# Moving projection groups inside a hybrid decoder layer: between the quarters of the merge, in pairs around the chain's steps, and a new order of the tail

## The chip, the cores and the metric

The kernel runs on one core of a Trainium2 chip. The metric is the device time of one execution in microseconds (us), as the median of several runs. TensorE does the matmuls and is PE in the rows; its weight loads are PEld. VectorE is DVE, ScalarE is ACT, GpSimd is POOL, and SyncE (SP) issues the transfers. TensorE's clock has two levels, 2.4 GHz and 1.2 GHz, and the profile gives the granted share: 1.00 is the full clock, 0.50 the half clock.

## The reference

One decoder layer on x of 512 x 1024 in float32. One input projection feeds two groups of heads, whose outputs are gated, joined and projected back:

```python
h = rms_norm(x, g_pre[l])
proj = h @ w_in[l]                                   # 512 x 1024 times 1024 x 4224
y_r = rwkv7_time_mix(p_rwkv, ...)                    # 8 heads of 64: a recurrence over 512 steps
q, k, v = jnp.split(p_attn, 3, axis=-1)
y_a = moba_attention(q, k, v)                        # 8 heads of 64: causal softmax, ALiBi, blocks of 256
y = jnp.concatenate([y_r, y_a], axis=-1) * jax.nn.silu(gates)
o = y @ w_out[l]
x = x + rms_norm(o, g_post[l])
```

The recurrence of one RWKV head, with a 64 x 64 state S, is

```python
Sa = jnp.einsum('bhij,bhj->bhi', S, a_t)
S = S * w_t[:, :, None, :] + Sa[..., None] * b_t[:, :, None, :] + v_t[..., None] * k_t[:, :, None, :]
y = jnp.einsum('bhij,bhj->bhi', S, r_t)
```

At 512 positions and blocks of 256 the attention of a query sees every earlier block, so the kernel computes plain causal attention with ALiBi.

## The kernel before

**Products in three parts.** Every large product splits its operands in two rounded halves (`hi`, `lo`) and adds hi x hi, hi x lo and lo x hi. The input projection makes 128 output columns at a time for all 512 positions: over two halves of the 1024 rows, three products of four matmuls (128 x 128 weights, 512 columns). Such a set of four matmuls is called a **projection group**, P, here; in the rows it is `ps_p<-xhi_r,whi`, `ps_p<-xhi_r,wlo` or `ps_p<-xlo_r,whi`, 128x512 x4. Its weights arrive over SP's queue as `wraw`, ScalarE rounds them to `whi`, VectorE subtracts to `wlo`. `PLAN` lists the pieces in order: keys (k), receptances (r) and values (v) of the RWKV pairs, V of the attention, then queries (q), attention keys (c) and gates (G).

**The stages.** After the first projections comes the *preparation* (`rwkv_keys`, `rwkv_pairs`, `rwkv_values`; four pairs of heads each): `rwkv_keys` makes two rank products of 128x512 on `ps_c` (`ps_c<-qx,V_r`; called K), norms, four transposes and the tiles AR, BK, E; `rwkv_pairs` transposes BK into BT (four 128 x 128 transposes on `ps_r`, called TB) and multiplies BK with AR (eight matmuls on `ps_s`, called A), in two halves per pair. `rwkv_inverse` then inverts the 32 x 32 triangular blocks on VectorE, moves them through DRAM, and merges them into 64 x 64 blocks on TensorE: two quarters of 32 matmuls of 32x32 for the first product (`ps_c<-BK_f,Am_f`) and two for the second (`ps_c<-Am_f,BK_f`). This is the *merge*. `rwkv_chain` walks eight chunks of 64 positions in sequence. A step of it runs on TensorE: F, 16 matmuls `ps_s<-E,AR_f` and `ps_r<-E,AR_f` that need the state of the step before; a copy of their result on ScalarE and one on VectorE; u, 8 matmuls `ps_c<-UV_f,Am_f`; copies of u; X, 16 matmuls `ps_s`/`ps_r<-UV_f,Am_f` that prepare the next chunk; D, 8 matmuls `ps_c<-UV_f,BT_f`, which needs the copies of u and gives the next state; Y, 8 matmuls of the output. The trace records each of these small float32 matmuls (32x32, 64x64, 64x128) as two, so that F has x32 there and the first product of the merge x128. Then follow the norm (`rwkv_norm`), the attention of four pairs of heads (`attn_pair`: scores, the row maxima on VectorE at L707, exponentials on ScalarE at L736, products with the values), the gating (`gates`, `gated`) and the output projection. The output is made in nine pieces, each from two **half** outputs of 12 matmuls: `half(i, 0)` over the RWKV heads and `half(i, 1)` over the attention heads.

**What sets the order.** The order of TensorE's instructions is written by a small planner at build time. `stream(projections())` emits one projection group at a time; after each, `side` lets other generators (the flows) emit a step, at most three per group, and at most two once the chain has ended. A flow says with `yield ns, wait` how much TensorE time the planner books for what it has just emitted and how long after that it wants not to be called. If no projection may be emitted, `drain` lets the clock jump to the earliest flow and takes one step at a time. `PENDING` is how many pieces past `q1` may be emitted before the chain has ended. These times are the planner's only; they make no wait on the chip. The engines run their instructions in the order written, and wait only for data and for buffers: PSUM banks are rings by tag (`PS`: two "p", three "s", two "c", one "r").

**The end.** `out_weights` brings the output weights (two of 256 KB per call of `wout`); `early_out` gates the RWKV heads and emits `half(0, 0)` and `half(1, 0)` among the attention; after all flows have ended, `half(i, 0)` of pieces 2 to 4 follow, and then the loop over the pieces, which emits `half(i + 5, 0)` ahead of `half(i, 1)`, sums squares on ScalarE (L910) and multiplies by g_post on VectorE (L913).

Of the kernel before, what the change touches and what calls it, by code (L numbers as in the profile page):

```python
# [39 lines left out]
PLAN = "k1 r1 k2 r2 k3 r3 v1 v2 v3 V q0 c0 G4 G5 q1 c1 q2 c2 G6 q3 c3 G7 G0 G1 G2 G3"  # L40
PENDING, AHEAD = 8, 5
MM = 232.0
# [3 lines left out]
def hybrid_layer(ctx, tc, x, xt, params, ranks, w_in, w_v, w_out, g_post, out):  # L46
# [53 lines left out]
    clock, flows, ready = [0.0], [], {}  # L100
# [258 lines left out]
    def rwkv_keys(p, ps):  # L359
# [4 lines left out]
        nc.scalar.activation(sq, k, AF.Square, scale=col(KK + p))  # L364
        yield 0, 0 if p else 4000
        th = []
# [23 lines left out]
        nc.scalar.activation(en, L, AF.Exp, scale=-1.0)  # L390
        yield 4 * MM, 5500

# [30 lines left out]
    def rwkv_pairs(p, ps):  # L423
# [7 lines left out]
        nc.vector.tensor_mul(ar[:, :, 1, :], v3(r), E[:, :, 1:C + 1])  # L431
        yield 0, max(4000, since[p] + 13000 - clock[0])
        msk = flat(mask).unsqueeze(1).to_broadcast([128, 4, 128])
        for c0 in (0, 4):
            ps = mps("r")
            for c in range(4):
                tr(ps[:, 128 * c:128 * c + 128], flat(BK[:, c0 + c]))
            acp(bt[:, c0:c0 + 4, :], ps.rearrange("p (c n) -> p c n", c=4))
            yield 900, 0
            pe = [mps("s") for _ in range(2)]  # L440
            for c in range(4):
                for e in range(2):
                    h = slice(64 * e, 64 * e + 64)
                    mm(pe[e][:, 128 * c:128 * c + 128], flat(BK[h, c0 + c]), flat(ar[h, c0 + c]), start=True, stop=True)
            for e in range(2):
                nc.vector.tensor_mul(am[:, e, c0:c0 + 4].rearrange("p c a b -> p c (a b)"),
                                     pe[e].rearrange("p (c n) -> p c n", c=4), msk)
            if c0:
                for hf in range(2):
                    d = slice(32 * hf, 32 * hf + 32)  # L450
                    nc.sync.dma_start(bd[hf, p].rearrange("n s t -> s n t"),
                                      am[d, :, :, 0, d].rearrange("s e c t -> s (e c) t"))
                paired[p] = True
            yield 1800, 2200
# [27 lines left out]
    def rwkv_inverse():  # L482
# [31 lines left out]
        for g in range(2):  # L514
# [6 lines left out]
            for e in range(2):  # L521
                (acp, vcp)[e](xq[32:64, 2 * g:2 * g + 2, e], px[64 * e + 32:64 * e + 64])
            yield 1700, 0
        for g in range(2):
# [6 lines left out]
            for q in range(2):  # L531
                for e in range(2):
                    (acp, vcp)[e](Am[2 * g + q][0:32, e, :, 0, 32:64], px[64 * e:64 * e + 32, q])
            yield 1700, 0
        ready["inverse"] = True
# [6 lines left out]
    def rwkv_chain():  # L542
# [20 lines left out]
        for c in range(NCH):  # L563
# [7 lines left out]
            vcp(uv[lo, 1], ry[1][hi])  # L571
            yield 900 * (c > 0), 700
            u = mps()[:, 0:NP * HD].rearrange("p (q i) -> p q i", i=HD)
# [4 lines left out]
            if not last:  # L578
                rn = values_in(c + 1)
            yield 500 + 1000 * (not last), 100  # L580
            if not last:
# [226 lines left out]
    def out_weights():  # L808
        for k in range(8):
            while not attended(*(((0, 1),) * 4 + ((0, 1, 2),) * 2 + ((0, 1, 2, 3),) * 2)[k]):  # L810
                yield 0, 300
            wout(k)
            ready["wout"] = k
            yield 0, 1500

# [17 lines left out]
    def early_out():  # L833
# [5 lines left out]
        for p in range(NP):  # L839
            gated(p, bonus[p])  # L840
        yield 0, 8000
        for i in range(2):
# [53 lines left out]
    for b in range(NB):  # L896
# [3 lines left out]
        os = [at() for _ in range(2)]  # L900
        for j, i in enumerate(mine):
            if i + AHEAD < len(pieces):
                for n in half(i + AHEAD, 0):
                    pass
            for n in half(i, 1):
                pass
            cs = slice(*pieces[i][1])
# [74 lines left out]
```

## Time and profile before

| | |
|---|---|
| runs | 385.98, 386.14, 391.16 us; median 386.14 us |
| profiled execution | 386.54 us, of which the span of its instructions is 384.8 us |
| granted TensorE clock over the span | 0.964 |
| busy | PE 358.9 us (93%), DVE 243.7 (63%), ACT 189.3 (49%), POOL 32.8 (9%) |
| transfers | 31.93 MB, mean 83 GB/s |
| projection groups in the stream | 600 matmuls `ps_p`, 58.3 + 57.9 + 56.9 us busy |
| chain that ended last | PE 80%, ACT 7%, DVE 6%, issue 3% |

The busy times are sums over the whole span; the engine that waits changes from stage to stage, so that the stages have to be read one by one. Matmuls overlap in the records: of four matmuls of 128x512 the row shows about 1.08 us, and the next row starts 0.92 us after it.

### The profile page before, as it was taken

What the parts mean: (1) busy time and instruction counts of PE and PEld (TensorE: products, weight loads), DVE (VectorE), ACT (ScalarE), POOL (GpSimd) and SP (SyncE); (2) the same over time, 40 slices, a digit from 0 to 9 for tenths busy, and PEclk for the clock granted to TensorE, in tenths of its full rate; (3) what the DMA queues carried; (4) which work ended last, traced back from release to release, by engine and by line L of the source; (5) the groups of instructions that cost most, each with busy time, mean ns of one, the idle gap of its engine ahead of it and who ended that gap; (6) DMA issues with size and microseconds to landing.
All of it is one profiled execution on the core that took longest, in us unless ns stands there. A gap on an engine that the chain in (4) does not pass through costs nothing.

```text
span 384.8 us, 7040 instructions
## 1 busy us (share of the span) xinstructions
PE 358.9 (93%) x2765; PEld 287.1 (75%) x2765; DVE 243.7 (63%) x521; ACT 189.3 (49%) x351; POOL 32.8 (9%) x55
## 2 busy tenths in 40 slices
PE   7999798999999999989999998889999989799893
PEld 3688576888877888877777775668888867688783
DVE  5976579859985999723544456884657961520344
ACT  5948855666654344632332357756457263510322
POOL 6000130012000000300000006222200000000000
PEclk9999998999999999976999996999999999989997
DMA  6830121321243223832111100110124401220334
GB/s 196 326 112 26 55 56 44 72 103 47 71 115 81 99 62 106 205 98 56 55 43 46 56 29 31 55 55 29 55 81 138 139 0 36 96 89 2 106 111 137
DMA packets 28321, 31.93 MB, mean 83 GB/s; under 512 B 12608, under 2 KB 15424, under 8 KB 28288
## 3 DMA queue, kind: packets, MB, share of 16 engines
q1 hardware_dynamic: 28288, 31.49, 27.0%
q8 instruction: 21, 0.34, 0.4%
q14 instruction: 12, 0.10, 0.1%
HBM read 28.07 MB, written 3.41 MB: 82 GB/s over the span
## 4 chain that ended last, share of the span: by engine, by line
PE 80%; ACT 7%; DVE 6%; issue 3%; DMA 1%; SPq 1%; POOL 1%; DVEq 0%; ACTq 0%
PE ps_p L92 38%; PE ps_s L92 23%; PE ps_c L92 12%; PE ps_r L92 4%; PE ps_r L95 3%; DMA AR_f<-in_xt_dram 1%; ACT t L736 1%; ACT BT_r L82 1%; DVE at L707 1%; PE ps_c L95 1%; DVE wlo L231 1%; POOL n L325 1%; ACT whi L82 1%; ACT BK_f L82 0%; SPq L153 0%
## 5 line engine op out<-in xcount | busy, mean ns | idle before, releaser
L92 PE MATMUL ps_p<-xhi_r,whi 128*128 128x512 f32 x200 | 58.3, 415 | 0.0
L92 PE MATMUL ps_p<-xlo_r,whi 128*128 128x512 f32 x200 | 57.9, 412 | 0.0
L92 PE MATMUL ps_p<-xhi_r,wlo 128*128 128x512 f32 x200 | 56.9, 407 | 0.0
L82 ACT ACTIVATE whi<-wraw 128x512 fp32r<-128x512 f32 x58 | 36.3, 628 | 39.1 <-PE ps_p L92 21.6
L231 DVE TENSOR_TENSOR wlo<-wraw,whi 128x512 fp32r<-128x512 f32 x58 | 39.9, 687 | 20.0 <-ACT whi L82 18.6
L92 PEld LDWEIGHTS ps_p<-xhi_r,whi 128*128 128x128 f32 x200 | 37.4, 196 | 7.8 <-issue 0.2
L92 PEld LDWEIGHTS ps_p<-xlo_r,whi 128*128 128x128 f32 x200 | 37.1, 195 | 7.6
L92 PEld LDWEIGHTS ps_p<-xhi_r,wlo 128*128 128x128 f32 x200 | 36.4, 191 | 7.4
L92 PE MATMUL ps_c<-V_f,t 128*128 128x65 f32 x160 | 22.7, 273 | 1.4 <-ACT t L736 1.4
L92 PEld LDWEIGHTS ps_c<-V_f,t 128*128 128x128 f32 x160 | 21.1, 192 | 3.1 <-ACT t L736 2.5
L736 ACT ACTIVATE t<-ps_s,alibi 128x512 f32<-128x512 f32 (+3 forms) x32 | 16.2, 523 | 10.6 <-PE ps_s L92 10.3
L92 PE MATMUL ps_s<-UV_f,Am_f 64*64 64x64 f32 x288 | 16.4, 238 | 0.0
L92 PEld LDWEIGHTS ps_s<-UV_f,Am_f 64*64 64x64 f32 x288 | 14.1, 150 | 1.2 <-issue 0.7
L82 ACT ACTIVATE Am_r<-wraw 128x512 fp32r<-128x512 f32 x16 | 9.9, 625 | 10.0 <-PE ps_s L92 6.0
L707 DVE CUSTOM_DVE_ANT_0 at<-ps_s,dist 128x128 f32<-128x128 f32 (+3 forms) x32 | 14.4, 486 | 0.4 <-PE ps_s L92 0.2
L803 DVE TENSOR_TENSOR UV_r<-wraw,Am_r 128x512 fp32r<-128x512 f32 x8 | 5.5, 685 | 14.2 <-ACT Am_r L82 14.2
L82 ACT ACTIVATE UV_f<-ps_c 64x512 f32<-64x512 f32 (+1 forms) x16 | 7.8, 485 | 13.6 <-PE ps_c L92 9.3
L325 POOL TENSOR_TENSOR n<-n,cols 128x8 f32<-128x8 f32 x4 | 7.8, 1943 | 75.5 <-DVE n L398 69.3
L92 PE MATMUL ps_s<-Am_r 128*128 128x128 f32 (+3 forms) x32 | 11.5, 367 | 1.4 <-ACT t L736 1.4
L92 PE MATMUL ps_p<-xhi_r,Am_r 128*128 128x512 f32 x32 | 10.9, 411 | 1.2 <-DVE Am_r L258 0.6
L82 ACT ACTIVATE t<-t,omm 128x512 f32<-128x512 f32 x13 | 9.3, 720 | 5.4 <-DVE t L319 4.6
L319 DVE TENSOR_TENSOR t<-ps_p,rinv 128x512 f32<-128x512 f32 x11 | 7.4, 681 | 5.7 <-PE ps_p L92 3.6
(305 smaller groups left out, 736.0 us busy)
## 6 DMA issues: line engine op xcount, KB each, us to landing
wraw<-in_w_in_dram SPq DMA_DIRECT2D x50, 256.0 KB, 2.9
wraw<-in_w_out_dram SPq DMA_DIRECT2D x16, 256.0 KB, 2.8
wraw<-in_w_v_dram SPq DMA_DIRECT2D x8, 256.0 KB, 3.0
wraw<-in_x_dram SPq DMA_DIRECT2D x8, 256.0 KB, 3.8
out_dram<-at SPq DMA_DIRECT2D x7, 256.0 KB, 2.0
AR_f<-in_xt_dram SPq DMA_DIRECT2D x4, 256.0 KB, 4.4
BT_f<-in_xt_dram SPq DMA_DIRECT2D x4, 256.0 KB, 6.3
BQ_f<-in_w_in_dram SPq DMA_DIRECT2D x4, 256.0 KB, 5.6
```

The lines of the kernel that those rows point to most:

```text
L82: nc.scalar.activation(out, in_, AF.Copy, scale=scale)
L92: return tc.keep_in_program_order(nc.tensor.matmul(*args, **kw))
L95: return tc.keep_in_program_order(nc.tensor.transpose(out, in_, ident))
L231: eng.tensor_sub(lo, raw, hi.bitcast(F32))
L319: nc.vector.tensor_mul(q, ps, rinv)
L325: nc.gpsimd.tensor_tensor(y, x, cols[:, 3:4].to_broadcast(list(x.shape)), ALU.pow)
L707: nc.vector.tensor_tensor_reduce(at()[:, 0:n], ps[:, 0:n], dist[:, i:i + b + 1, :].rearrange("p j s -> p (j s)"), -1.0, 3.0e38, ALU.add, A ...
L736: nc.scalar.activation(PT[j][:, 0:n], ps[:, 0:n], AF.Exp, scale=2.0 ** -(h + 1), bias=alibi[:, h, j:j + 1])
L803: nc.vector.tensor_sub(lo, raw, hi.bitcast(F32))
```

## The change

Only the order in which the instructions are emitted changes, with one exception: the second A of each pair takes one of its two PSUM banks from the ring "c" in place of "s". The amounts of work and the transfers are the same. The diff, without its unchanged lines:

```diff
-PENDING, AHEAD = 8, 5
+PENDING, AHEAD = 9, 5
@@ rwkv_keys
-        yield 0, 0 if p else 4000
+        yield 0, 0 if p else 5000
@@ rwkv_keys, after the rank products
-        yield 4 * MM, 5500
+        yield 4 * MM, 6500
@@ rwkv_pairs
-        yield 0, max(4000, since[p] + 13000 - clock[0])
+        yield 0, max(4000, since[p] + (13000 if p else 15000) - clock[0])
...
-            pe = [mps("s") for _ in range(2)]
+            pe = [mps("s"), mps("c" if c0 else "s")]
@@ rwkv_inverse, the merge, in both of its loops
-            yield 1700, 0
+            yield 1700, 500
@@ rwkv_chain, after F
-            yield 900 * (c > 0), 700
+            yield 900 * (c > 0), 1000
@@ rwkv_chain, after u and X
-            yield 500 + 1000 * (not last), 100
+            yield 500 + 1000 * (not last), 0 if not last else 700
@@ out_weights
-            yield 0, 1500
+            yield 0, 4000 if k < 4 else 1500
@@ early_out
         for p in range(NP):
             gated(p, bonus[p])
-        yield 0, 8000
+            yield 0, 3000
+        yield 0, 3000
         for i in range(2):
             for n in half(i, 0):
                 yield 4 * MM, 0
@@ the loop over the pieces
+            for n in half(i, 1):
+                pass
             if i + AHEAD < len(pieces):
                 for n in half(i + AHEAD, 0):
                     pass
-            for n in half(i, 1):
-                pass
```

**The preparation, TensorE**, around the first transposes of BK. `ps_c<-ident,t` are the transposes of the norms (L95) of pair 0 and pair 1, `ps_r<-ident,BK_f` is TB and `ps_s<-AR_f,BK_f` is A of pair 0. Before:

```order
L95 MATMUL ps_c<-ident,t 128x128 x4
L92 MATMUL ps_p<-xhi_r,wlo 128x512 x4
L95 MATMUL ps_c<-ident,t 128x128 x4
L92 MATMUL ps_p<-xlo_r,whi 128x512 x4
L92 MATMUL ps_p<-xhi_r,whi 128x512 x4
L92 MATMUL ps_p<-xhi_r,wlo 128x512 x4
L92 MATMUL ps_p<-xlo_r,whi 128x512 x4
L95 MATMUL ps_r<-ident,BK_f 128x128 x4
L92 MATMUL ps_s<-AR_f,BK_f 128x128 x8
```

After:

```order
L95 MATMUL ps_c<-ident,t 128x128 x4
L92 MATMUL ps_p<-xlo_r,whi 128x512 x4
L95 MATMUL ps_c<-ident,t 128x128 x4
L92 MATMUL ps_p<-xhi_r,whi 128x512 x4
L92 MATMUL ps_p<-xhi_r,wlo 128x512 x4
L92 MATMUL ps_p<-xlo_r,whi 128x512 x4
L92 MATMUL ps_p<-xhi_r,whi 128x512 x4
L92 MATMUL ps_c<-qx,V_r 128x512 x4
L92 MATMUL ps_p<-xhi_r,wlo 128x512 x4
L95 MATMUL ps_r<-ident,BK_f 128x128 x4
L92 MATMUL ps_s<-AR_f,BK_f 128x128 x8
```

The two rank products K of the next pair of heads stand ahead of TB now (x4 in the listing: each is two matmuls), and two more projection groups stand between the start of the program and TB, one of them next to K.

**The merge, TensorE**, from the last projection group ahead of it to the first `u` of the chain. `ps_s<-UV_f,Am_f` is X of the first chunk. The listing counts the matmuls as the code emits them. Before:

```order
L92 MATMUL ps_p<-xhi_r,whi 128x512 x4
L92 MATMUL ps_c<-BK_f,Am_f 32x32 x64
L92 MATMUL ps_c<-Am_f,BK_f 32x32 x32
L92 MATMUL ps_p<-xhi_r,wlo 128x512 x4
L92 MATMUL ps_c<-Am_f,BK_f 32x32 x32
L92 MATMUL ps_s<-UV_f,Am_f 64x64 x16
L92 MATMUL ps_p<-xlo_r,whi 128x512 x4
L92 MATMUL ps_p<-xhi_r,whi 128x512 x4
L92 MATMUL ps_c<-UV_f,Am_f 64x64 x8
```

After:

```order
L92 MATMUL ps_p<-xhi_r,whi 128x512 x4
L92 MATMUL ps_c<-BK_f,Am_f 32x32 x32
L92 MATMUL ps_p<-xhi_r,wlo 128x512 x4
L92 MATMUL ps_c<-BK_f,Am_f 32x32 x32
L92 MATMUL ps_p<-xlo_r,whi 128x512 x4
L92 MATMUL ps_c<-Am_f,BK_f 32x32 x32
L92 MATMUL ps_p<-xhi_r,whi 128x512 x4
L92 MATMUL ps_c<-Am_f,BK_f 32x32 x32
L92 MATMUL ps_p<-xhi_r,wlo 128x512 x4
L92 MATMUL ps_s<-UV_f,Am_f 64x64 x16
L92 MATMUL ps_p<-xlo_r,whi 128x512 x4
L92 MATMUL ps_p<-xhi_r,whi 128x512 x4
```

The four quarters of the merge now have a projection group between each two; there are five groups from the first row to X where there were two.

**A step of the chain, TensorE**, from the group before u to D. Before (the second chunk):

```order
L92 MATMUL ps_p<-xhi_r,wlo 128x512 x4
L92 MATMUL ps_c<-UV_f,Am_f 64x64 x8
L92 MATMUL ps_s<-UV_f,Am_f 64x64 x16
L92 MATMUL ps_p<-xlo_r,whi 128x512 x4
L92 MATMUL ps_c<-UV_f,BT_f 64x64 x8
```

After (the second chunk):

```order
L92 MATMUL ps_p<-xhi_r,whi 128x512 x4
L92 MATMUL ps_p<-xhi_r,wlo 128x512 x4
L92 MATMUL ps_c<-UV_f,Am_f 64x64 x8
L92 MATMUL ps_s<-UV_f,Am_f 64x64 x16
L92 MATMUL ps_c<-UV_f,BT_f 64x64 x8
```

The projection group between X and D now stands ahead of u, next to the other one.

**The last attention pairs, VectorE**: the row maxima (L707) and the gating of the RWKV heads (L783, L785) with the last gates (L776, L778). Before:

```order
L783 SCALAR_TENSOR_TENSOR at<-bonus_381,AR_f 128x512
L776 TENSOR_TENSOR t<-ps_p,rinv 128x512
L783 SCALAR_TENSOR_TENSOR at<-bonus_382,AR_f 128x512
L785 TENSOR_TENSOR xlo_r<-at,xhi_r 128x512
L778 SCALAR_TENSOR_TENSOR E<-E,t 128x512
L785 TENSOR_TENSOR xlo_r<-at,xhi_r 128x512
L783 SCALAR_TENSOR_TENSOR at<-bonus_383,E 128x512
L783 SCALAR_TENSOR_TENSOR at<-bonus_384,E 128x512
L707 ISA at,mx<-ps_s,dist 128x384
L707 ISA mx 128x1
L785 TENSOR_TENSOR xlo_r<-at,xhi_r 128x512 x2
L707 ISA at,mx<-ps_s,dist 128x512
```

After:

```order
L707 ISA at,mx<-ps_s,dist 128x128
L707 ISA mx 128x1
L707 ISA at,mx<-ps_s,dist 128x256
L707 ISA mx 128x1
L707 ISA at,mx<-ps_s,dist 128x384
L707 ISA mx 128x1
L707 ISA at,mx<-ps_s,dist 128x512
L707 ISA mx 128x1
L783 SCALAR_TENSOR_TENSOR at<-bonus_381,AR_f 128x512
L783 SCALAR_TENSOR_TENSOR at<-bonus_382,AR_f 128x512
L785 TENSOR_TENSOR xlo_r<-at,xhi_r 128x512 x2
```

All the maxima of the last pair now stand ahead of the gating.

On TensorE as a whole the number of projection groups is 150 in both. In the changed order two more of them stand ahead of the first F of the chain, three more ahead of the first attention score, and none where three of them stood among the last attention pairs. The halves of pieces 0 and 1 over the RWKV heads have left the attention and stand after it.

## Rows read from the trace of the kernel before

**Rows 1.** the windows view: busy time by engine, TensorE clock, DMA share, GB/s.

```profile
60.00:70.00 10.00, 10.00 (x80) 7.97 (x80) 10.00 (x17) 5.07 (x9) 0.00 (x0) 0.84 0.16 52
170.00:180.00 10.00, 9.89 (x153) 8.40 (x154) 3.62 (x7) 2.62 (x6) 0.00 (x0) 0.54 0.21 56
230.00:240.00 10.00, 8.39 (x79) 6.16 (x74) 5.75 (x10) 7.22 (x15) 5.84 (x13) 0.69 0.09 29
300.00:310.00 10.00, 8.56 (x48) 6.68 (x46) 9.73 (x30) 4.16 (x7) 0.00 (x0) 1.00 0.41 134
```

**Rows 2.** timeline, preparation: start, length, instruction [idle before it, its releaser].

```profile
55.94 1.07 PE L92 MATMUL ps_p<-xlo_r,whi 128*128 128x512 f32 x4
...
59.00 0.74 DVE L407 SCALAR_TENSOR_TENSOR yt<-t,prm,ps_c 128x512 f32<-128x512 f32 x1
...
59.13 0.66 PE L95 MATMUL ps_r<-ident,BK_f 128*128 128x128 f32 x4 [2.12 <-DVE BK_f L418]
```

**Rows 3.** timeline of PE, the merge and the first chain step.

```profile
164.10 2.21 PE L92 MATMUL ps_c<-BK_f,Am_f 32*32 32x32 f32 x128
...
166.71 1.20 PE L92 MATMUL ps_c<-Am_f,BK_f 32*32 32x32 f32 x64 [0.40 <-DVE BK_f L85]
...
170.11 1.92 PE L92 MATMUL ps_c<-Am_f,BK_f 32*32 32x32 f32 x64 [1.07 <-DVE Am_f L85]
...
171.96 1.97 PE L92 MATMUL ps_s<-UV_f,Am_f 64*64 64x64 f32 x32
...
184.06 0.27 PE L92 MATMUL ps_s<-E,AR_f 64*64 64x64 f32 x1
```

**Rows 4.** timeline, one step of the chain, 206 to 215 us.

```profile
206.82 0.69 PE L92 MATMUL ps_s<-E,AR_f 64*64 64x64 f32 x32
...
208.57 0.51 PE L92 MATMUL ps_c<-UV_f,Am_f 64*64 64x64 f32 x10
...
209.35 0.38 ACT L82 ACTIVATE UV_f<-ps_c 64x256 f32<-64x256 f32 x1 [1.42 <-PE ps_c L92]
...
209.76 0.43 DVE L85 COPY UV_f<-ps_c 64x256 f32<-64x256 f32 x1 [1.40 <-ACT UV_f L82]
...
209.94 1.19 PE L92 MATMUL ps_p<-xlo_r,whi 128*128 128x512 f32 x4
...
211.06 0.69 PE L92 MATMUL ps_c<-UV_f,BT_f 128*64 128x64 f32 x16
...
214.33 0.27 PE L92 MATMUL ps_s<-E,AR_f 64*64 64x64 f32 x1
```

**Rows 5.** timeline, end of the chain, 227 to 237 us.

```profile
227.03 2.59 ACT L82 ACTIVATE BT_r<-t 64x512 fp32r<-64x512 f32 x4 [1.84 <-PE ps_c L92]
...
232.82 0.36 ACT L82 ACTIVATE UV_f<-ps_s 64x256 f32<-64x256 f32 x1
...
233.24 0.68 PE L92 MATMUL ps_c<-UV_f,Am_f 64*64 64x64 f32 x16 [1.61 <-ACT UV_f L82]
...
236.90 1.65 PE L92 MATMUL ps_p<-xhi_r,whi 128*128 128x512 f32 x3
```

**Rows 6.** timeline, last attention pairs, 306 to 316 us.

```profile
306.14 0.69 DVE L783 SCALAR_TENSOR_TENSOR at<-bonus,AR_f 128x512 f32<-128x512 f32 x1
...
309.90 0.44 PE L92 MATMUL ps_s<-Am_r 128*128 128x384 f32 x1 [1.44 <-ACT t L736]
...
311.21 0.55 DVE L707 CUSTOM_DVE_ANT_0 at<-ps_s,dist 128x384 f32<-128x384 f32 x1
...
313.63 0.68 DVE L707 CUSTOM_DVE_ANT_0 at<-ps_s,dist 128x512 f32<-128x512 f32 x1
...
315.46 1.11 PE L92 MATMUL ps_c<-V_f,t 128*128 128x65 f32 x8 [0.30 <-ACT t L736]
```

**Rows 7.** the chain that ended last: the two early half outputs.

```profile
317.60 5.53 PE ps_p L92 x24
```

**Rows 8.** PE's waits: us in total, times, longest; the last stage.

```profile
PE ps_s L92 <- DVE at L913: 1.6, 1, 1.6
```

More of the change, by code (lines that the diff above doesn't have):

```diff
@@ L533, in rwkv_inverse @@
                     (acp, vcp)[e](Am[2 * g + q][0:32, e, :, 0, 32:64], px[64 * e:64 * e + 32, q])
-            yield 1700, 0
+            yield 1700, 500
         ready["inverse"] = True
```

## The prediction

> **What bounds the kernel now.** I read the windows first, for the stages in which PE is not full or its clock is not 1.00, then the timeline inside each. PE is busy 93% of the span and most of the chain that ended last, so a gain has to come from idle PE, from PE at the half clock, or from nowhere. Four stages of ten us stand out [rows 1]. In 60 to 70 the clock is 0.84, which makes 3.2 us at half clock and 1.6 us lost; DVE is full there. In 170 to 180, the merge and the start of the chain, PE is 9.89 busy, but at 0.54: 9.2 us at half clock, 4.6 us lost. In 230 to 240, the end of the chain, PE is 8.39 busy at 0.69: 1.6 us idle and 3.1 us lost, part of it in time that PE would have waited. In 300 to 310 the clock is full, PE is 8.56 busy and DVE 9.73. What came before each fall is in the timelines: 2.12 us idle in the preparation [rows 2]; in the merge a stretch of 32x32 matmuls from 164.10 to 167.84 with only 0.40 us idle in it, then 1.07 idle [rows 3]; 1.61 us idle at the end of the chain [rows 5].
>
> **The change part by part** (a plus is time won, against the profiled 386.54 us).
>
> *Preparation, -0.5.* TB waits for BK, the DVE instruction L418, and starts at 59.13; ahead of it lie 2.12 us of idle PE [rows 2]. In the changed order K and two P more stand ahead, 3 x 0.92 = 2.8 us of work that is done later in the kernel before, so TB at 61.9 would be even. But K's second product needs the "c" bank that DVE's L407 of the second pair frees. L407 stands behind L418, and two more weight subtractions stand ahead of that; instructions of that shape start 0.60 apart on the full DVE (58.40 to 59.00 is one), so L407 ends at about 59.74 + 1.2 = 60.9. Then half of K (0.46), a P (0.92) and TB at 62.4: 0.5 late, with 2.6 us idle in place of 2.12, and the clock falls as before. Bounds: two P in place of one hidden and the fall gone, +1.6; the fall lasting twice as long, -2.
>
> *Merge to the first F, +3.1.* Before, 164.10 to 184.06, 19.96 us with six P [rows 3]. After, with eight: first product 2.21 + second product 2 x 1.13 (166.71 to 167.84, full clock) + four P among small matmuls at 1.12 (209.94 to 211.06 [rows 4]) 4.48 + X at full clock 0.95, half of the 1.90 from 171.96 to the next row (its own 1.97 includes the overlap) + two pairs of P at 2.05 each 4.10 + u and X 1.37 (208.57 to 209.94) + D's wait of 0.25, priced below + D and Y 1.23. Sum 16.85, so F at 181.0, and two P more are already done; those show below as missing work. The copies between the quarters (idle 0.40 and 1.07) take less than a P of 1.12, so they are hidden. Against it: if the clock falls here all the same, one fall of the size seen in 60 to 70 costs 1.6, and two 3.2, which is the lower bound of this term; the upper is +3.5, without D's wait.
>
> A rule of the Trainium skill speaks to this term: the page "TensorE: Matmul & The Clock Gate", section "HAM oscillation — how this bites in real kernels", puts such falls down to the gaps in which PE idles between bursts. The rows differ, since PE was idle only 0.40 us in the stretch ahead of the fall; by the page the filled gaps alone keep the clock and the term stands; by the rows a fall can follow small matmuls without a gap, and the term loses 1.6 for each.
>
> *Six steps of the chain, -0.3.* A step takes 7.51 us (206.82 to 214.33), four P in it [rows 4]. Two single P cost 1.13 + 1.12; as a pair they cost 2.05 (as 182.01 to 184.06 in the trace, where two stand together): 0.2 won. D needs both copies of u, ACT's (209.35, 0.38) and DVE's behind it (209.76, 0.43), which end at 210.19; X ends at 209.94. The P that covered these 0.25 us is gone, so D waits: 0.25 lost. Net -0.05 a step. Bounds: DVE has other work in front of its copy, as it has between 206 and 208, at 0.3 more a step, -2; the copy comes earlier, +1.2.
>
> *End of the chain, +0.6.* PE's 1.61 us of idle end with ACT's copy at 232.82, which waits behind four copies BT_r (2.59 us, 0.65 each) and what follows them [rows 5]. One more P now stands there. If all the idle goes, +1.6; but ACT has two AR_r copies and a whi (about 3 x 0.65 = 1.9) between the two halves of the last state, of which one P (0.92) covers half: -1.0.
>
> *Attention start, -0.5.* ACT's second BQ_r copy stands behind two more ACT instructions of 0.65: 0 to -1.3, and DVE is the full engine around it, so less than half of it counts.
>
> *Late attention, +3.2.* At 309.90 PE has waited 1.44 us for an exponential, though three "s" banks are there [rows 6]: two of them hold scores whose maxima DVE takes only at 311.21 and 313.63, behind ten instructions of the gating and the gates, the first of them L783 at 306.14. In the changed order all the maxima stand ahead of these. DVE is full up to there, so the maximum of 311.21 moves to 306.14 at the earliest and its bank is free at 306.14 + 0.55 = 306.7. PE needs that bank at 309.90 - 1.44 - 2.8 = 305.7, since three P (3 x 0.92 = 2.8 us), done by now in the merge and the chain, have left the stretch from 300 to 306. So the scores of 309.90 start at 306.7: 3.2 won, of at most 2.8 + 1.44 = 4.2. The lower bound is 0, if PE then waits for DVE or ACT in the place where the three P were.
>
> *The moved halves, -1.4.* Two early halves take 5.53 us on the chain that ended last [rows 7]; they cost the same where they stand now. Where they stood, they covered ACT's exponentials; without them a wait of the kind of 0.30 at 315.46 [rows 6] comes once more, and the gating's two last ACT copies of 0.65 now stand among the last head's exponentials: 0.4 + 1.0. Bounds 0 and -3.
>
> *Tail, +1.6.* One wait of 1.6 us for L913, the multiplication that frees the "s" bank of an earlier piece [rows 8]. With `half(i, 1)` first, 2.8 us of other work (half of 5.53) stands between; gone. If another bank is late in its place, 0.
>
> The transfers, the bank "c" for A, and `PENDING` of nine by itself: 0; the queue of SP keeps its order but for two weight loads that come two places earlier, and DMA is busy 0.09 to 0.41 in the four windows. Without that room a late weight would stop a P for the length of a load.
>
> Sum: -0.5 + 3.1 - 0.3 + 0.6 - 0.5 + 3.2 - 1.4 + 1.6 = 5.8 us. 386.54 - 5.8 = 380.7 us; the median of the runs is 0.4 below the profiled execution, so **380.3 us**.
>
> **The rivals.**
> 1. *The late attention keeps its time.* There the three P are cover: take them away and PE waits for the exponentials and DVE (9.73 busy in 300 to 310) instead. For it speaks that DVE is full there with them; against it that ten DVE instructions leave the place. Then +3.2 becomes 0: 383.5 us, and 385.1 if the moved halves lose their bound of 3 too.
> 2. *The preparation stops waiting.* If K and the P fill the 2.12 us because DVE's order lets L407 go in time, the idle of 2.6 goes, and with it the fall that cost 1.6: 4.2 us more, 376.1 us. Against it stands DVE's full row in 60 to 70.
> 3. *Slower: the chain loses its clock.* u, X, D and Y now run without a P among them, 1.37 + 0.25 + 1.23 = 2.85 us of small matmuls in each step; before, the P between split this in two. The merge shows a fall behind a stretch of small matmuls with hardly a gap. If the chain's stretches do the same, each fall costs the 1.6 us of 60 to 70; four of them use up the 5.8, and seven cost 11.2: 391.5 us. Against it: two pairs of P stand around each stretch, and the chain's steps before have had none. By the skill's page it would not come, as PE idles only 0.25 us in it.
> 4. *The order does little:* each wait only moves to the next place, 386 us.
>
> **How the numbers follow.** Forecast 0.50 (377.5 to 382.5), rival 1 0.25 (382.5 to 387), rival 2 0.15 (373.5 to 377.5), rival 3 0.06 (387 to 395), rival 4 0.04. The range 374.5 to 387 leaves out rival 3 and the lower end of rival 2, with something of the term bounds. Two per cent, about what a measurement of this kernel tells from no change, is 7.7 us: under 378.4 counts as faster. That takes in rival 2 and a third of the forecast's lower part, 0.30; over 393.9 is the far end of rival 3, 0.03; the rest, 0.67, is within.
>
> **What the profile after would show.** 170 to 180 at a clock near 1.00 and no idle between the merge's quarters; F of the first step some 3 us earlier; a wait of about 0.25 us of D for UV_f in each step; TB at about 62.4 behind a wait of K for L407; L707's last maximum ahead of the first L783 and no wait of 1.4 us at the first exponentials of the last two pairs; five halves in a row after the attention; no wait for L913. I am wrong if the clock falls in the merge or in the chain, or if the exponentials' waits between 300 and 335 grow by what the three groups gave back.

## The result and the profile after

The changed kernel took 382.19 us in the median of four executions (380.43 to 383.75), the kernel before 386.16 us (385.98 to 391.16). The ratio is 0.989 with a 95% interval of 0.984 to 0.994: faster by 1.1%, inside the range on record and 1.9 us over the predicted 380.3. It is also inside the two per cent that the prediction counts as no change. The profiled execution of the changed kernel is the slowest of its four, 383.75 us with a span of 381.9, so that the trace has 2.9 us to explain.

The windows of the changed kernel (busy time of PE, PEld, DVE, ACT, POOL; TensorE clock; DMA share; GB/s), against [rows 1]:

```profile
60.00:70.00 10.00, 8.79 (x53) 7.07 (x54) 8.42 (x14) 5.32 (x10) 0.00 (x0) 0.68 0.09 28
170.00:180.00 10.00, 10.00 (x235) 7.84 (x230) 5.29 (x10) 4.40 (x10) 0.00 (x0) 1.00 0.23 72
230.00:240.00 10.00, 9.07 (x92) 6.85 (x92) 5.87 (x10) 8.87 (x17) 6.27 (x14) 1.00 0.17 57
300.00:310.00 10.00, 8.84 (x54) 6.67 (x52) 9.59 (x33) 3.80 (x7) 0.00 (x0) 1.00 0.26 94
```

The merge went from clock 0.54 to 1.00 and the end of the chain from 0.69 to 1.00. The preparation got worse, 0.84 to 0.68 with PE no longer full, and the late attention stands where it stood: DVE 9.59 busy, PE 8.84.

Timeline of PE in the preparation and the merge of the changed kernel, against [rows 2, 3]:

```profile
61.22 1.19 PE L92 MATMUL ps_c<-qx,V_r 128*128 128x512 f32 x2 [3.64 <-DVE yt L407]
62.21 1.91 PE L92 MATMUL ps_p<-xhi_r,wlo 128*128 128x512 f32 x4
63.91 1.05 PE L95 MATMUL ps_r<-ident,BK_f 128*128 128x128 f32 x4
...
166.67 1.20 PE L92 MATMUL ps_c<-BK_f,Am_f 32*32 32x32 f32 x64
...
183.75 0.27 PE L92 MATMUL ps_s<-E,AR_f 64*64 64x64 f32 x1
```

K's second product waits 3.64 us for L407, and TB stands at 63.91, where 62.4 was forecast. In the merge no wait is left, and from its start to the first F it takes 183.75 - 166.67 = 17.08 us for eight groups; before it took 19.96 for six, and 16.85 were forecast.

Timeline of PE in a chain step and in the late attention of the changed kernel, against [rows 4, 6]:

```profile
196.04 0.68 PE L92 MATMUL ps_c<-UV_f,BT_f 128*64 128x64 f32 x14 [0.27 <-DVE UV_f L85]
...
308.41 0.42 PE L92 MATMUL ps_s<-Am_r 128*128 128x384 f32 x1
...
310.29 0.36 PE L92 MATMUL ps_s<-Am_r 128*128 128x256 f32 x1
...
329.94 1.11 PE L95 MATMUL ps_r<-ident,t 128*128 128x128 f32 x4 [1.20 <-DVE t L745]
330.71 2.05 PE L92 MATMUL ps_p<-Am_r,xhi_r 128*128 128x512 f32 x4
```

D's small wait is there (0.27). The scores that waited 1.44 us at 309.90 start at 308.41 without a wait. The last transposes, those of the last pair's outputs, wait 1.20 us for L745, the VectorE instruction that writes the last of what they transpose, and the first of the moved halves behind them (330.71) runs at the half clock, 2.05 us for what takes 1.07 otherwise.

Three rows of PE in the kernel before, for the table below: the first transposes of the maxima, the third scores of the fifth head, and the last transposes:

```profile
255.43 0.60 PE L95 MATMUL ps_r<-ident,mx 128*1 128x128 f32 x4
...
311.32 0.38 PE L92 MATMUL ps_s<-Am_r 128*128 128x256 f32 x1
...
336.11 1.00 PE L95 MATMUL ps_r<-ident,t 128*128 128x128 f32 x4 [1.20 <-DVE t L745]
```

The waits of PE in the changed kernel (us in total, times, longest) name what is late now:

```profile
PE ps_c L92 <- DVE yt L407: 4.0, 2, 3.6
PE ps_s L92 <- DVE mx L707: 3.1, 3, 1.8
PE ps_c L92 <- ACT t L736: 3.0, 7, 1.0
```

The wait for L913 [rows 8] has left the list; those for L407 (none before), L707 (1.5 before) and L736 at the value products (1.4 before) have grown.

The same places in both traces cut the span into seven pieces (plus is time won). Each number is of one execution; the section on the prediction's steps sets the other traces beside them.

| piece | before | after | won | forecast |
|---|---|---|---|---|
| start to the merge | 164.10 | 166.67 | -2.6 | -0.5 |
| merge to the first F | 19.96 | 17.08 | +2.9 | +3.1 |
| six chain steps, first to seventh F (229.80; 230.10) | 45.74 | 46.35 | -0.6 | -0.3 |
| to the first transposes of the maxima (255.43; 255.27) | 25.63 | 25.17 | +0.5 | +0.1 |
| to the third scores of the fifth head (311.32; 310.29) | 55.89 | 55.02 | +0.9 | +3.2 |
| to the last transposes (336.11; 329.94), the two halves (5.55) taken out of before | 19.24 | 19.65 | -0.4 | -1.4 |
| to the end, the halves taken out of after | 48.69 | 46.41 | +2.3 | +1.6 |

The sum is 3.0 of the 2.9 us; the forecast was 5.8. The merge is as forecast, but the preparation and the late attention are 4.4 us short of theirs, and the tail and the halves 1.7 us better. The fall of the clock at the end of the chain has not gone but moved: the clock is 1.00 from 185 to 240 us of the changed kernel and 0.83 from 240 to 250, behind a wait of 1.84 us for L707.

### The profile page after: what moved, and what is told of

Its sections match the earlier page's. It is cut to its first block, busy times and chain, and to the rows that moved or that the text cites. A ratio compares the mean times of both kernels' runs of the same rounds, so it can differ in the third digit from the quotient of the medians.

```text
span 381.9 us, 7041 instructions
## 1 busy us (share of the span) xinstructions
PE 354.6 (93%) x2765; PEld 284.0 (74%) x2765; DVE 245.2 (64%) x521; ACT 188.6 (49%) x351; POOL 31.9 (8%) x55
## 4 chain that ended last, share of the span: by engine, by line
PE 53%; ACT 7%; DVE 4%; issue 2%; POOL 1%; DVEq 0%; ACTq 0%
PE ps_p L92 23%; PE ps_s L92 16%; PE ps_c L92 9%; PE ps_r L92 4%; ACT Am_r L82 2%; PE ps_r L95 2%; ACT t L736 1%; ACT BT_r L82 1%; POOL gn L325 1%; ACT UV_r L82 1%; ACT whi L82 1%; DVE at L707 1%; ACT BK_f L82 0%; DVE wlo L231 0%; DVE AR_r L682 0%
## 5 line engine op out<-in xcount | busy, mean ns | idle before, releaser
L92 PE MATMUL ps_p<-xlo_r,whi 128*128 128x512 f32 x200 | 56.1, 402 | 0.0
L92 PE MATMUL ps_p<-xhi_r,whi 128*128 128x512 f32 x200 | 55.7, 400 | 0.0
L92 PEld LDWEIGHTS ps_p<-xhi_r,whi 128*128 128x128 f32 x200 | 36.1, 188 | 7.2
L92 PEld LDWEIGHTS ps_p<-xlo_r,whi 128*128 128x128 f32 x200 | 35.9, 188 | 7.3
L736 ACT ACTIVATE t<-ps_s,alibi 128x512 f32<-128x512 f32 (+3 forms) x32 | 16.0, 522 | 8.4 <-PE ps_s L92 8.2
L92 PE MATMUL ps_s<-UV_f,Am_f 64*64 64x64 f32 x288 | 14.8, 222 | 0.3 <-ACT UV_f L82 0.3
L707 DVE CUSTOM_DVE_ANT_0 at<-ps_s,dist 128x128 f32<-128x128 f32 (+3 forms) x32 | 14.1, 487 | 0.5 <-PE ps_s L92 0.2
L92 PEld LDWEIGHTS ps_s<-UV_f,Am_f 64*64 64x64 f32 x288 | 12.5, 134 | 1.6 <-ACT UV_f L82 0.7
L321 DVE SCALAR_TENSOR_TENSOR t<-t,prm 128x511 f32<-128x511 f32 x13 | 9.6, 748 | 2.8 <-ACT t L82 2.7
L914 DVE TENSOR_TENSOR at<-ps_p,yt 128x512 f32<-128x512 f32 x2 | 1.4, 686 | 15.3 <-ACT t L911 15.3
```

Of the source, the lines that this page charges most:

```text
L92: return tc.keep_in_program_order(nc.tensor.matmul(*args, **kw))
L321: nc.vector.scalar_tensor_tensor(t[:, 1:T], q[:, 0:T - 1], col(MU + m), t[:, 1:T], ALU.mult, ALU.add)
L707: nc.vector.tensor_tensor_reduce(at()[:, 0:n], ps[:, 0:n], dist[:, i:i + b + 1, :].rearrange("p j s -> p (j s)"), -1.0, 3.0e38, ALU.add, A ...
L736: nc.scalar.activation(PT[j][:, 0:n], ps[:, 0:n], AF.Exp, scale=2.0 ** -(h + 1), bias=alibi[:, h, j:j + 1])
L914: nc.vector.tensor_mul(os[cs.start // 512][:, cs.start % 512:cs.start % 512 + w], ps, gpb[:, cs])
```

## The experiments

The time of this kernel moves by some us between executions with the share of half clock in them (the changed kernel: 380.43 us at a mean clock of 0.998, 383.75 at 0.980), so medians are given with their ratio to the kernel before, and places are compared inside the traces.

**1. The merge alone.**

```diff
-            yield 1700, 0
+            yield 1700, 500
```
(in both loops of the merge, nothing else of the change)

> The kernel before with the merge edit alone. Theory 1 (the merge wins about 2.9 us up to the first F, but the three projection groups that are then missing in the attention were cover there, so that waits for the maxima and the exponentials give back most of it): first F at about 181.2 us with two groups more, total 384.5 to 386. Theory 2 (the win goes through to the end): total 380.5 to 383.3.

Measured: median 393.23 us, ratio 1.012 (1.007 to 1.017). It is slower than the kernel before, beyond both theories. Timeline of PE in this kernel at the late maxima:

```profile
313.74 0.79 PE L92 MATMUL ps_s<-Am_r 128*128 128x512 f32 x1 [3.78 <-DVE mx L707]
```

Timeline of its DVE at the same place, from the first instruction of the gating to the first maximum behind it:

```profile
309.14 1.29 DVE L783 SCALAR_TENSOR_TENSOR at<-bonus,AR_f 128x512 f32<-128x512 f32 x2
...
313.39 0.28 DVE L707 CUSTOM_DVE_ANT_0 at<-ps_s,dist 128x128 f32<-128x128 f32 x1
```

Its window of the 20 us from there:

```profile
310.00:330.00 20.00, 16.26 (x62) 13.03 (x63) 6.32 (x17) 6.56 (x12) 0.00 (x0) 0.66 0.00 0
```

With the three groups gone, PE reaches the last maxima while the gating still stands ahead of them on DVE: it waits 3.78 us, and the clock is at 0.66 over the 20 us from there, 13.6 us at half clock. So the groups were cover there, and without the other edits more than the win is lost. The profiled execution took 396.88 us, 3.7 over the median, so that this fall may be longer than in most. (The early halves also come two value products earlier in this order, behind the wait.)

**2. The merge and the output weights.**

```diff
-            yield 1700, 0
+            yield 1700, 500
@@ out_weights
-            yield 0, 1500
+            yield 0, 4000 if k < 4 else 1500
```

> The merge edit and the longer times between the output weights together. Theory (the merge alone was slow because the last maxima, behind the gating, kept PE waiting 3.8 us and the clock fell behind that): no such wait, 1.5 to 4 us under the kernel before. Rival (the merge edit costs at another place, as the 2.9 us wait at the end of the chain): at the kernel before or over it.

Measured: median 387.13 us, ratio 1.000 (0.996 to 1.004). The wait of 3.78 us is gone, since the gating now follows the maxima. But no time is won against the kernel before; the end of the chain waits 2.91 us, as it does in experiment 1, for 1.61 in the kernel before [rows 5]:

```profile
232.45 0.80 PE L92 MATMUL ps_c<-UV_f,Am_f 64*64 64x64 f32 x10 [2.91 <-ACT UV_f L82]
```

Both theories hold a half: the wait is repaired, and the rival's time came.

**3. The output weights alone.**

```diff
-            yield 0, 1500
+            yield 0, 4000 if k < 4 else 1500
```

> The kernel before with the longer times between the output weights alone, which by the order put the gating of the RWKV heads behind the last maxima and the two early halves behind the attention. Theory (the late maxima held PE's banks): no wait of 1.4 us in the last two pairs, 1.5 to 3 us under the kernel before. Rival (the halves and the gating were cover there and PE now waits for exponentials instead): 0 to 1 us over it.

Measured: median 387.03 us, ratio 0.998 (0.994 to 1.002), nothing that can be told from no change. The wait of 1.44 us at the scores is gone, and one of 1.48 us for an exponential stands behind its place, with the clock at 0.83 over 310 to 330:

```profile
315.17 1.17 PE L92 MATMUL ps_c<-V_f,t 128*128 128x65 f32 x8 [1.48 <-ACT t L736]
```

The two halves did not land behind the attention here, as the expectation has it: without the other edits they stand behind the transposes of the third pair.

**4. The changed kernel without the merge's edit.**

```diff
-            yield 1700, 500
+            yield 1700, 0
```

> The changed kernel with the merge edit undone. Theory 1 (the attention gives the merge's win back): within 1 us of the changed kernel, 381.5 to 383.2 us. Theory 2 (the win goes through): about 2.9 us more, 385 us.

Measured: median 381.0 us, ratio 0.986 (0.981 to 0.992). The time fits theory 1, being no longer than that of the changed kernel, but does not show it. In this order the early halves come one value product ahead of the last transposes, and from the third scores of the fifth head to the end its trace takes 379.4 - 310.55 = 68.85 us where the changed kernel's takes 381.9 - 310.29 = 71.61. This second difference is about as large as the merge's 2.9 us and can hide them; experiments 5 and 6 are without it.

**5 and 6. The changed kernel without the preparation's edits, with and without the merge's.** Both have the halves directly ahead of the last transposes, so that the merge's edit is their one difference. (`PENDING` is 9 in the fifth and 8 in the sixth; the sixth's instructions are the same with either.)

```diff
-        yield 0, 0 if p else 5000
+        yield 0, 0 if p else 4000
...
-        yield 4 * MM, 6500
+        yield 4 * MM, 5500
...
-        yield 0, max(4000, since[p] + (13000 if p else 15000) - clock[0])
+        yield 0, max(4000, since[p] + 13000 - clock[0])
...
-            pe = [mps("s"), mps("c" if c0 else "s")]
+            pe = [mps("s") for _ in range(2)]
@@ in the sixth also, in both loops of the merge
-            yield 1700, 500
+            yield 1700, 0
```

> The changed kernel with the four edits of the preparation undone. Theory (the preparation costs 2.6 us by the wait of K for L407 and the fall of the clock behind it): the merge starts at 164.1 us instead of 166.7, total about 2.6 us under the changed kernel, 379.6 us. Rival (the time is absorbed later, as the later stages are not bound by PE): total as the changed kernel, 382.2 us, or less than 1 us under it.

> The changed kernel without the edits of the preparation and without that of the merge. Theory 1 (the merge's win is given back in the attention): within 1 us of the changed kernel without the preparation's edits, so 0.979 to 0.984 of the kernel before. Theory 2 (it goes through): 2.9 us more, 0.987 to 0.992.

Measured: 378.78 us, ratio 0.981 (0.977 to 0.985), and 378.73 us, ratio 0.979 (0.974 to 0.984). The merge's edit is worth nothing here, and the traces show where it goes. Windows of the kernel with the merge's edit, at the merge and in the attention:

```profile
170.00:180.00 10.00, 10.00 (x241) 7.88 (x240) 5.61 (x11) 3.81 (x9) 0.00 (x0) 1.00 0.22 63
254.30:305.60 51.30, 48.28 (x296) 39.60 (x295) 33.28 (x77) 28.04 (x50) 6.53 (x4) 1.00 0.26 83
```

Timeline of its PE, the first F, the first transposes of the maxima and a later pair's:

```profile
182.84 0.27 PE L92 MATMUL ps_s<-E,AR_f 64*64 64x64 f32 x1
...
254.35 0.60 PE L95 MATMUL ps_r<-ident,mx 128*1 128x128 f32 x4
...
305.75 0.49 PE L95 MATMUL ps_r<-ident,mx 128*1 128x128 f32 x3
```

The same windows of the kernel without the edit:

```profile
170.00:180.00 10.00, 9.56 (x125) 7.37 (x126) 4.04 (x8) 2.76 (x7) 0.00 (x0) 0.50 0.10 28
254.60:305.70 51.10, 50.37 (x310) 41.86 (x309) 34.34 (x83) 27.42 (x49) 7.42 (x4) 1.00 0.26 83
```

And the timeline of its PE:

```profile
184.68 0.27 PE L92 MATMUL ps_s<-E,AR_f 64*64 64x64 f32 x1
...
254.62 0.60 PE L95 MATMUL ps_r<-ident,mx 128*1 128x128 f32 x4
...
305.66 0.60 PE L95 MATMUL ps_r<-ident,mx 128*1 128x128 f32 x4
```

The merge runs at 1.00 in place of 0.50, and the kernel with the edit is at the first F 1.84 us earlier with three more groups done. At the first transposes of the maxima it still has the three groups, but only 0.27 us, 254.35 and 254.62: the stretch from the seventh F to there takes it 25.13 us for 23.89. At 305.7 both are at the same point again: the kernel with the edit has the three groups, 12 matmuls, fewer to do in the 51 us between, and is no faster. Its PE is idle for 51.30 - 48.28 = 3.0 us there, the other's for 51.10 - 50.37 = 0.7. The waits that are new are 0.98 us for an exponential at 272.30 and 0.78 for a maximum at 302.90, and one of 0.73 for a copy of maxima became 1.18.

**7. The changed kernel with K behind TB.**

```diff
-        yield 4 * MM, 6500
+        yield 4 * MM, 5500
```

> The changed kernel with one time of the preparation undone (5500 in place of 6500), by which K stands behind TB again, with the other times as changed. Theory (the preparation loses by K's wait for L407 alone): no wait at K, 2 to 3 us under the changed kernel, 0.979 to 0.985 of the kernel before. Rival (it loses by the later L418, whoever stands first): TB waits as long as K did, 0.987 to 0.991.

Measured: median 383.38 us, ratio 0.991 (0.988 to 0.995). My theory fell: no wait at K, but no time won. PE of this kernel waits at TB and A instead, 2.1 us in both, and the clock falls there all the same:

```profile
64.16 0.63 PE L95 MATMUL ps_r<-ident,BK_f 128*128 128x128 f32 x4 [1.47 <-DVE BK_f L417]
64.72 0.49 PE L92 MATMUL ps_s<-AR_f,BK_f 64*128 64x128 f32 x2
65.87 2.07 PE L92 MATMUL ps_s<-AR_f,BK_f 64*128 64x128 f32 x14 [0.67 <-DVE Am_f L446]
```

It is VectorE that sets the time of this stage, 9.62 us busy of the ten from 60 to 70; whoever stands first on PE waits for it. But this order has a second difference, the halves directly ahead of the last transposes as in experiment 8, and from the merge on its order on TensorE is that of experiment 8. The two differ ahead of the merge: it starts at 169.65 us here, at 165.53 there and at 166.67 in the changed kernel. So K behind TB, with the other times as changed, costs some 3 to 4 us in the trace (there are later waits for VectorE too, 1.30 us at 113.3 with a fall of the clock behind it), 3.2 in the medians, and the place of the halves, 381.8 - 313.30 = 68.50 us from the third scores of the fifth head to the end for 71.61, gives them back.

**8 and 9. The place of the two early halves.** In the changed kernel they stand behind the last transposes, in experiments 5 and 6 ahead of them. One number of `early_out` moves them: from behind to ahead in the changed kernel, from ahead to behind in the kernel of experiment 6. On TensorE nothing else moves; on VectorE and ScalarE a split of the output weights changes place with its neighbour.

```diff
@@ early_out, after the gating; experiment 8
-        yield 0, 3000
+        yield 0, 2000
@@ experiment 9, on the kernel of experiment 6
-        yield 0, 3000
+        yield 0, 5000
```

> The changed kernel with the two early halves directly ahead of the last four transposes of the attention instead of behind them; no other instruction of TensorE moves. Theory 3 (the place of these halves decides: there they hide the 1.2 us that the transposes wait for L745, and the fall of the clock behind that wait): 2 to 3 us under the changed kernel, 0.981 to 0.985 of the kernel before. Rival (the preparation alone makes the changed kernel slower than its version without the preparation's edits): no difference, 0.987 to 0.992.

> The changed kernel without the edits of the preparation and the merge, with the two early halves moved behind the last transposes. Theory 3: the 1.2 us wait for L745 comes back and with it the fall, 2 to 3 us over the same kernel with the halves ahead, 0.983 to 0.988 of the kernel before. Rival: no difference, 0.976 to 0.982.

Measured: 380.17 us (379.9 to 381.99), 2.0 under the changed kernel, ratio 0.977 (0.968 to 0.985); and 380.9 us (378.87 to 383.35), 2.2 over experiment 6, ratio 0.977 (0.964 to 0.989). The runs of the kernel before beside these scatter from 385.32 to 393.60, so that the ratios are wide and say less than the medians. Experiment 8, PE at the end of the attention:

```profile
332.49 0.62 PE L92 MATMUL ps_p<-BT_r,xhi_r 128*128 128x512 f32 x2
332.95 0.60 PE L95 MATMUL ps_r<-ident,t 128*128 128x128 f32 x4
```

Its window there:

```profile
325.00:335.00 10.00, 9.48 (x50) 8.04 (x51) 4.17 (x9) 3.67 (x8) 0.00 (x0) 1.00 0.34 107
```

Experiment 9, the same place:

```profile
328.65 1.12 PE L95 MATMUL ps_r<-ident,t 128*128 128x128 f32 x4 [1.20 <-DVE t L745]
329.42 2.05 PE L92 MATMUL ps_p<-Am_r,xhi_r 128*128 128x512 f32 x4
```

Its window there:

```profile
325.00:335.00 10.00, 8.46 (x42) 7.13 (x41) 4.38 (x8) 3.55 (x7) 0.00 (x0) 0.83 0.34 107
```

Ahead, the halves take the place of the 1.20 us wait and the clock stays at 1.00; behind, the wait is there and the clock is 0.83 over ten us, 1.7 us lost: together 2.9, of which the medians show 2.0 and 2.2. Both signs are as theory 3 has them, and the traces show the wait and the fall come and go with the place. The executions of the two kernels of each pair overlap, so that the medians alone do not settle the size. The traces do for their executions: from the third scores of the fifth head to the end experiment 8 takes 378.2 - 309.12 = 69.08 us for 71.61 in the changed kernel, and experiment 9 380.7 - 309.53 = 71.17 for 377.8 - 309.30 = 68.50 in experiment 6, 2.5 and 2.7 us. All 14 profiled kernels agree on the wait: in the five with the halves directly ahead of these transposes (experiments 5 to 8 and 12) it is gone, in eight of the nine others it is 1.20 us, in experiment 4 it is 0.73. A fall of the clock follows seven of the eight waits of 1.20 us, and neither the 0.73 nor the five without a wait.

**10. The tail alone.** The order of the last loop as in the change, nothing else.

```diff
-            if i + AHEAD < len(pieces):
-                for n in half(i + AHEAD, 0):
-                    pass
             for n in half(i, 1):
                 pass
+            if i + AHEAD < len(pieces):
+                for n in half(i + AHEAD, 0):
+                    pass
```

> The kernel before with the order of the last loop alone. Theory: the wait of 1.6 us for L913 goes and nothing comes in its place: 384.6 us. Rival: another bank is late in its place, 386.1 us.

Measured: median 386.29 us against 387.31, ratio 0.999 (0.994 to 1.003). The trace agrees with the theory, no wait stands at the place of [rows 8] or near it; the 1.6 us are too few to be told from nothing in the times.

**11. The chain alone.**

```diff
-            yield 900 * (c > 0), 700
+            yield 900 * (c > 0), 1000
...
-            yield 500 + 1000 * (not last), 100
+            yield 500 + 1000 * (not last), 0 if not last else 700
```

> The kernel before with the two times of the chain alone. Theory (the win is at the chain's end, where the longer time at the last step puts more projection groups under the wait of 1.6 us for UV_f): that wait is gone and the clock holds there in most executions, 1 to 3 us under the kernel before, 0.992 to 0.997. As the prediction had it (a step costs 0.05 more, the end wins 0.6): 0.998 to 1.001.

Measured: 384.37 us (384.09 to 385.84), ratio 0.987 (0.979 to 0.996), some 2 us under the kernel before. The end of its chain, against [rows 5]:

```profile
232.26 0.68 PE L92 MATMUL ps_c<-UV_f,Am_f 64*64 64x64 f32 x16 [0.15 <-ACT UV_f L82]
```

The wait of 1.61 us is 0.15. The six steps take 229.34 - 183.27 = 46.07 us against 45.74: the pairs of groups cost 0.3 us. From the seventh F to the first transposes of the maxima it is 23.96 us for 25.63, with one group more done. But most of this is not the edit's. Experiments 3, 10 and 12 keep the chain of the kernel before, with waits of 1.59 to 1.62 us at the same place; none of them has the fall behind it, and they take 24.42 to 24.56 us. Experiment 12, its wait on PE:

```profile
233.16 0.68 PE L92 MATMUL ps_c<-UV_f,Am_f 64*64 64x64 f32 x16 [1.62 <-ACT UV_f L82]
```

Its window there:

```profile
230.00:240.00 10.00, 8.27 (x90) 6.24 (x80) 6.36 (x11) 8.27 (x17) 7.22 (x16) 1.00 0.12 39
```

So the fall of the kernel before at 230 to 240 [rows 1] can come or stay away with the wait there, and the 2 us of the medians are not all the edit's.

**12. The late edits without the chain's.** The kernel before with `early_out`, `out_weights` and the tail as in the change; the halves stand ahead of the last transposes.

```diff
-            yield 0, 1500
+            yield 0, 4000 if k < 4 else 1500
@@ early_out
-        yield 0, 8000
+            yield 0, 3000
+        yield 0, 3000
@@ and the order of the last loop, as in experiment 10
```

> The kernel before with the edits of early_out, out_weights and the tail, without those of the chain, the merge and the preparation; the halves stand ahead of the last transposes. Theory: what is left of the win without the chain's edits, 4 to 6 us under the kernel before, 0.984 to 0.990. Rival (the chain's edits are worth nothing beside it): 0.977 to 0.981 as with them.

Measured: 379.27 us (379.12 to 381.86), ratio 0.975 (0.966 to 0.984). The rival: nearly the whole win of experiment 6 (378.73 us) is here; the 0.5 us between the medians cannot be told from nothing. In the medians, of different sets of runs, these three edits alone stand 2.9 us under the changed kernel (379.12 to 381.86 us against 380.43 to 383.75). Experiments 4, 5, 6, 8, 9 and 12 have lower medians than both kernels; between 5, 6 and 12 the runs show no difference.

## Why the prediction was right, and where its steps were not

The total was right within its range, with errors that cancel, and so in part by luck: of the 5.8 us forecast 4.0 came in the medians, and the step with the largest share, the late attention, failed.

*Preparation.* The order of events was right: K waits for L407, with VectorE as the bound, and the clock falls. Inside it the sizes were not. L407 ended at 61.07 for 60.9, but PE came there a us earlier than I counted, since a wait of 1.44 us for L372 at 45.77 in the kernel before is 0.41 in the changed one; so the idle was 3.64 us, not 2.6. Half of K and the group behind it then ran at the half clock, which I had left out: TB at 63.91. Yet what the edits cost up to the merge is near the forecast, and the -2.6 of the table is mostly an early start in the one trace of the kernel before. Nine other kernels (experiments 1 to 3, 5, 6 and 9 to 12) run the same instructions as it up to the merge; in these ten traces the merge starts at 163.97 to 166.33 us, 165.6 in the mean. In the three with the changed order (the changed kernel, experiments 4 and 8) it starts at 165.53 to 166.67, 166.0 in the mean: 0.4 later, for 0.5 forecast. On TensorE experiments 5 and 8 differ in the preparation alone; their medians stand 1.4 us apart, 378.78 and 380.17, in different sets of runs, and the merge starts at 165.76 and 165.53. So it stays open whether the preparation costs anything; most of the 3.4 us between the medians of the changed kernel and experiment 5 is the place of the halves, 2.5 to 2.7 us in the traces.

*Merge.* Right in mechanism. In all eight profiled kernels without this edit the clock over 165 to 185 is 0.74 to 0.83, in all six with it 1.00. The size, +2.9 for +3.1, is that of a trace in which the half clock lasted long. The six groups take 19.27, 19.29 and 17.89 us in experiments 3, 10 and 12, which have the order of the kernel before there (the last with the clock at 0.83), so that the edit, with the two groups that it brings ahead, won 0.8 to 2.9 us.

*Chain.* The step's cost was right (-0.6 for -0.3, with the wait of 0.27 for 0.25). At the end the wait of 1.61 us went, as forecast, and the size was about right: +0.5 for +0.1 in the trace. From the merge's start to the first transposes experiments 11 and 12, with and without the chain's edits, have as many groups and, by their windows, the same 10.2 us at the half clock; they take 87.3 and 88.1 us, 0.8 won for +0.3 forecast of the steps and the end. The kernel before takes 91.3 there, with 17 us at the half clock.

*Late attention.* This is the step that failed: +3.2, measured +0.9. Its first half is right: the maxima move ahead of the gating, the bank comes free, and the wait of 1.44 us goes. The other half, that the three groups missing there are 2.8 us won, is wrong. The traces part the two, in the piece from the first transposes of the maxima to the third scores of the fifth head, at the full clock in all of them:

| gating of the last pair | groups | kernels | us |
|---|---|---|---|
| ahead of the maxima | there | before, experiments 10 and 11 | 55.85 to 55.97 |
| behind them | there | experiments 3, 4, 6, 9 and 12 | 54.68 to 54.99 |
| behind them | three taken away, with the merge's edit | the changed kernel, experiments 2, 5, 7 and 8 | 55.01 to 55.05 |

The fourth case, ahead of the maxima and with the groups taken away, is experiment 1: 60.82 us, with its wait of 3.78 us and the half clock. So the order of the maxima won some 1.2 us, and taking the groups away won nothing. I took the stretch as bound by PE up to the wait. Experiments 5 and 6 show that the 12 matmuls fewer turn into 2.3 us more idle PE, waiting for maxima and exponentials. That is rival 1, priced as if it would take the whole 3.2; it took the part of the groups. In the prediction's own rows DVE was 9.73 busy beside PE's 8.56, and I used that to bound the bank and not the whole stretch.

*Moved halves and tail.* -1.4 and +1.6 were forecast, -0.4 and +2.3 came. What I missed is a wait that the rows did not hold, L745 ahead of the last transposes, 1.20 us in the kernel before as well (336.11), with a fall of the clock behind it. Where the halves go decides whether it is covered, and the changed kernel sets them on the wrong side by one call of the planner.

*Rivals.* Rival 1 came in part, as said, and rival 4 (386 us) did not come. Rival 2 did not come; the wait in the preparation grew. Rival 3 did not come: the clock is 1.00 through the chain of the changed kernel, with its 2.85 us of small matmuls per step. The prediction names the Trainium skill's page "TensorE: Matmul & The Clock Gate", section "HAM oscillation — how this bites in real kernels"; by that rule the filled gaps keep the clock, and the trace agrees for the merge and the chain (1.00 in both). No run here has the small matmuls without gaps and without groups, so the two causes of the merge's fall are not told apart.

## What to carry to other kernels

Work that is moved forward to fill a gap is also taken away from the place where it stood. Before its time is booked as won, look at what it covered there: if another engine is full in that stretch, the time comes back as waits, and with a fall of the clock behind them it can come back larger. Then look for the waits that stand at the end of a stage, where nothing else is queued, and put movable work directly ahead of them: here two half outputs ahead of four transposes, one number in a planner, were worth about 2 us, and a merge at the full clock, 1.8 us and three groups ahead at the first F, was worth nothing at the end.

## What was not expected of the hardware

The same program runs with different stretches of half clock from one execution to the next, and its time follows: the changed kernel took 380.43, 380.90, 383.49 and 383.75 us at mean clocks of 0.998, 0.989, 0.980 and 0.980. The place changes too. In the profiled executions of experiments 5 and 6 the clock is down between 45 and 55 us, where it is 1.00 in the kernel before and the changed one, and up at 60, where both of these show the fall. The same holds of later falls. A wait of 1.83 to 1.85 us for L707 between 240 and 246 us stands in eleven of the 14 traces, and in eight of them the clock falls behind it (0.86 over 240 to 252), in three it stays at 1.00; experiments 6 and 9, with and without that fall, run the same instructions up to there. So a fall seen at one wait in one trace is not a fixed cost of that wait, and a term of 1.7 us for a fall should be booked with a chance. And one trace on each side does not price a stage: ten kernels with the same instructions up to the merge reach it at times 2.4 us apart.
